# Epsilon inside the sum of squares, or added by ScalarE: the normalizations between and after the stages of a streaming-encoder block

## The chip, the cores and the metric

The kernel runs on one core of a Trainium2 chip. A core has TensorE (PE, matrix products into PSUM), VectorE (DVE), ScalarE (ACT), GpSimd (POOL), SyncE (SP, which here only starts DMA transfers), and 16 DMA engines. The metric is the time of one execution on the device in microseconds (us), as a median over runs; lower is better.

## The reference, cut to what matters

The reference is one residual block over 256 tokens of width 2048: a half-step SwiGLU network, a mixer, and another half-step SwiGLU network. After each of the three stands a normalization with gain and bias, and ahead of each a normalization without them, modulated by a vector that depends on the condition c.

```python
def _layer_norm(x, gain=None, bias=None):
    xf = x.astype(jnp.float32)
    mu = xf.mean(-1, keepdims=True)
    var = jnp.square(xf - mu).mean(-1, keepdims=True)
    y = (xf - mu) * lax.rsqrt(var + LN_EPS)
    ...
def modulate(h, s):
    return _layer_norm(h) * (1.0 + scale[:, s, None, :]) + shift[:, s, None, :]

y = _swiglu(modulate(x, 0), ffn1_w13[l], ffn1_w2[l])
x = _layer_norm(ALPHA * x + FFN_WEIGHT * gate[:, 0, None, :] * y, ln_g[l, 0], ln_b[l, 0])
u = modulate(x, 1)
...
x = _layer_norm(ALPHA * x + gate[:, 1, None, :] * y, ln_g[l, 1], ln_b[l, 1])
y = _swiglu(modulate(x, 2), ffn2_w13[l], ffn2_w2[l])
x = _layer_norm(ALPHA * x + FFN_WEIGHT * gate[:, 2, None, :] * y, ln_g[l, 2], ln_b[l, 2])
```

Each of these needs the reciprocal root of a variance plus epsilon (1e-5), one number for each token. The change is about who adds that epsilon.

## The kernel before, in words

The 256 tokens are two tiles of 128, one token to a partition; in the code `t` is 0 or 1, and `x[:, t, :]` holds a tile's 2048 columns. Weights stream in from memory as tiles of 128 by 2048, ScalarE and VectorE split each into a high and a low part, and TensorE multiplies the parts; this goes on almost without a gap from start to end. Each engine has a queue of its own that it works through in order. Around the places here the order in each queue is the order of the code: `V`, `A`, `G`, `T` and `Q` stand for VectorE, ScalarE, GpSimd, TensorE and SyncE and record every operation at one line of a helper, so that the profile shows L359 for all of them, and tiles have to be told by their names. The second SwiGLU network is laid out by a planner, but not its last part.

`boundary` (L577) makes the way from one stage to the next. It is called three times: after the first network (L1164, s = 0), after the mixer (L1928, s = 1) and at the very end (L1621, s = 2). The first two are **passages**: there `following` holds what the next stage needs. At the **end** `following` is None.

In it `norm(t)` (L616) makes a tile's normalization with gain and bias. VectorE turns statistics into mean and variance (`mv`, in the profile mvp), and `rstd_in_order` (L570) makes the factor `r` (rsp) on GpSimd in two instructions: an addition of epsilon (to the tile vep) and a power with the exponent -0.5. Meanwhile VectorE computes (x - mean) * gain for four quarters of 512 columns (L633). Then four instructions multiply by `r` and add the bias (L638, L644).

In a passage the modulated normalization follows at once and needs the mean and variance of what was just made. L638 sums each quarter into a column of the tile `sq`, and ScalarE sums the squares (L641). L649 adds up four columns each (tot), L651 makes the mean of it, and L652 makes mean squared minus mean square, the negated variance. `rstd_in_order` with the sign -1 turns it round and adds epsilon in one instruction (ven), and takes the power (rsn). With it `n_of` (L661) makes the normalized quarters n; TensorE transposes them (tu), ScalarE modulates them (u), VectorE makes a copy of the high part, and TensorE goes on with the next stage's products (o after the first passage, f after the second). While a tile's statistics are due, TensorE still has products of the other tile (tl), and ahead of the first transposes a `warm` product with tot as an operand.

At the end the second tile has a short cut for two of its four quarters (`early`): TensorE adds the products x * gain and -mean * gain in PSUM (tz), the second from a diagonal (dm) that ScalarE makes of the negated mean (nbn); L644 then reads tz in place of x. Each quarter is stored as soon as it is made (L645).

Of the kernel before, what the change touches and what calls it, by code (L numbers as in the profile page):

```python
# [11 lines left out]
F32 = mybir.dt.float32  # L12
F32R = mybir.dt.float32r
AF = mybir.ActivationFunctionType
ALU = mybir.AluOpType

P = 128
# [11 lines left out]
EPS = 1e-5  # L29
# [253 lines left out]
def block_kernel(ctx: ExitStack, tc: tile.TileContext, a: dict, out: bass.AP):  # L283
# [5 lines left out]
    sm = ctx.enter_context(tc.tile_pool(name="sm", bufs=4))  # L289
# [74 lines left out]
    V, A, G, T, Q = (Pinned(e) for e in (nc.vector, nc.scalar, nc.gpsimd, nc.tensor, nc.sync))  # L364
# [202 lines left out]
            A.mul(x[:, t, :], x[:, t, :], ALPHA)  # L567


    def rstd_in_order(var, nm, sign=1.0):  # L570
        v = sm.tile([P, 1], F32, tag="ve", name="ve" + nm)
        G.tensor_scalar(v, var, sign, EPS, op0=ALU.mult, op1=ALU.add)
        r = sm.tile([P, 1], F32, tag="rs", name="rs" + nm)
        G.tensor_tensor(r, v, mhalf, op=ALU.pow)
        return r

    def boundary(s, ps, hls, order, mm, sts, following, gated=False):  # L577
# [9 lines left out]
        if following:  # L587
            tiles, nm, ready, in_slots, fill, has_time, turn_at = following
# [27 lines left out]
        def norm(t, early={}):  # L616

            mv = sm.tile([P, 2], F32, tag="mv", name=f"mvp{s}{t}")
            V.bn_aggr(mv, sts[t].rearrange("p a b -> p (a b)"))
            r = rstd_in_order(mv[:, 1:2], f"p{s}{t}")  # L620

            sq = sums[t] = sm.tile([P, 2, 4], F32, tag="sq", bufs=2, name=f"sq{s}{t}")
            if early:
                nm_ = sm.tile([P, 2], F32, tag="nb", name=f"nbn{s}{t}")
                A.mul(nm_[:, 0:1], mv[:, 0:1], -1.0)
                diag = sm.tile([P, 512], F32, tag="gy", bufs=2, name=f"dm{s}{t}")[:, 0:P]
                A.activation(diag, ident, AF.Copy, scale=nm_[:, 0:1])
                for n in early:
                    T.matmul(early[n], diag, g[:, cs[n]], start=False, stop=True)
            for n, c in enumerate(cs):  # L630
                if n in early:
                    continue
                V.scalar_tensor_tensor(x[:, t, c], x[:, t, c], mv[:, 0:1], g[:, c], op0=ALU.subtract, op1=ALU.mult)  # L633
                yield
            for n in sorted(range(4), key=lambda n: n in early):
                c = cs[n]
                if following:
                    V.scalar_tensor_tensor(x[:, t, c], x[:, t, c], r, b[:, c], op0=ALU.mult, op1=ALU.add,  # L638
                                           accum_out=sq[:, 0, n:n + 1])
                    junk = sm.tile([P, 512], F32, tag="gy" if t else "u", bufs=2, name=f"junk{s}{t}{n}")  # L640
                    A.activation(junk, x[:, t, c], AF.Square, bias=sbs, scale=D ** -0.5,  # L641
                                 accum_out=sq[:, 1, n:n + 1])
                else:
                    V.scalar_tensor_tensor(x[:, t, c], early.get(n, x[:, t, c]), r, b[:, c], op0=ALU.mult, op1=ALU.add)  # L644
                    nc.sync.dma_start(out[t * P:(t + 1) * P, c], x[:, t, c])  # L645
                yield
            if following:
                tot = tots[t] = sm.tile([P, 4], F32, tag="tot", bufs=2, name=f"tot{s}{t}")
                V.tensor_reduce(tot[:, 0:2], sq, op=ALU.add, axis=mybir.AxisListType.X)  # L649

                V.tensor_scalar(tot[:, 2:3], tot[:, 0:1], 1.0 / D, sb, op0=ALU.mult, op1=ALU.add)  # L651
                V.scalar_tensor_tensor(tot[:, 3:4], tot[:, 2:3], tot[:, 2:3], tot[:, 1:2], op0=ALU.mult,  # L652
                                       op1=ALU.subtract)
                r = rstd_in_order(tot[:, 3:4], f"n{s}{t}", -1.0)
                nm_ = sm.tile([P, 2], F32, tag="nb", name=f"nbn{s}{t}")
                A.activation(nm_[:, 0:1], tot[:, 2:3], AF.Identity, bias=sb, scale=-1.0)
                A.activation(nm_[:, 1:2], nm_[:, 0:1], AF.Copy, scale=r)
                mrb[t] = nm_[:, 0:1], r, nm_[:, 1:2]
                yield
# [64 lines left out]
        mrb, sums, tots = {}, {}, {}  # L724
# [9 lines left out]
        if not following:  # L734
            run(norm(0))
            with tc.issue_after(end.ins):
                for n in early:
                    T.matmul(early[n], ident, x[:, 1, cs[n]], start=True, stop=False)
            run(takes(1, order[1]))
            run(norm(1, early))  # L740
            return

        A.activation(b, b, AF.Identity, accum_out=sb)
        A.mul(sb, sb, -1.0 / D)
        A.mul(sbs, sb, D ** -0.5)
        one = norm(0)
        other = chain(takes(1, order[1]), norm(1))

# [1326 lines left out]
```

## Time and profile before

| What | Value |
| --- | --- |
| median of 3 runs | 1861.64 us |
| lowest and highest of them | 1860.46 and 1862.16 us |
| the profiled execution | 1859.48 us |
| its span, first to last instruction | 1857.7 us |
| busy: TensorE, VectorE, ScalarE, GpSimd | 1842.9, 1610.5, 932.0, 66.2 us |
| granted TensorE clock, mean | 0.999 of full speed |
| instructions of GpSimd | 94 |
| memory traffic over the span | 294 GB/s |

The profile records the start and length of each instruction in one execution, counted from the start of the span. A row of its timeline has the start, the length, the engine, the source line, the instruction, the tile that it writes, and after the arrow those that it reads, with the count of equal instructions in a row. In brackets stands how long the engine had been idle and what released it. The chain of waits goes back from the last instruction, at each step to what came last before it; an engine's share of it says how much of the span hung on that engine. SCALAR_TENSOR_TENSOR is an instruction of VectorE with two tensors and a number for each partition. The first passage lies at about 740 to 812 us, the second at about 1126 to 1170 us, the end from about 1838 us on.

### The profile page before, as it was taken

Reading aid. Unit: us, or ns where it says so; the run is one execution under the profiler, and the core shown is the slowest. Engines: PE = TensorE matmul, PEld = TensorE weight load, DVE = VectorE, ACT = ScalarE, POOL = GpSimd, SP = SyncE. Lnnn points to the kernel's source line nnn. Section 1 sums busy time; section 2 is a strip of 40 time slices with the busy share of each in tenths; the row PEclk is TensorE's granted clock in tenths of the full one; section 3 lists DMA queues with packets and bytes.
Section 4 is the critical chain, followed back from the end, with each engine's and each line's share of the span. In section 5 each row is a group of like instructions: output and inputs, shape, how many; then the busy total and the mean of one; then the engine's idle time right before and its main releaser. Section 6 shows DMA issues by size and latency. Waiting matters only on the chain.

```text
span 1857.7 us, 21314 instructions
## 1 busy us (share of the span) xinstructions
PE 1842.9 (99%) x8423; PEld 1511.5 (81%) x8423; DVE 1610.5 (87%) x1506; ACT 932.0 (50%) x874; POOL 66.2 (4%) x94
## 2 busy tenths in 40 slices
PE   8999999999999999999999999999999999999998
PEld 5788888888888888788888887888888888888886
DVE  6899998888887986889997778899999989989886
ACT  4533444534333335564844346766565655665550
POOL 0000000000000000100000021000000000000000
PEclk9999999999999999999999999999999999999999
DMA  9999889999999897368678654888988888888852
GB/s 376 416 363 355 323 317 345 349 345 354 348 366 362 336 345 271 157 259 287 264 281 310 239 207 191 317 287 249 316 298 279 312 247 312 277 255 280 276 226 91
DMA packets 78677, 547.34 MB, mean 295 GB/s; under 512 B 9153, under 2 KB 9329, under 8 KB 13937
## 3 DMA queue, kind: packets, MB, share of 16 engines
q1 hardware_dynamic: 72144, 507.54, 71.2%
q0 software_dynamic: 4704, 34.63, 9.1%
q10 hardware_dynamic: 1728, 3.80, 0.6%
q8 instruction: 66, 1.08, 0.2%
q14 instruction: 35, 0.28, 0.0%
HBM read 541.72 MB, written 4.22 MB: 294 GB/s over the span
## 4 chain that ended last, share of the span: by engine, by line
PE 93%; DVE 3%; DMA 1%; ACT 1%; issue 1%; POOL 0%; POOLq 0%; DVEq 0%; SPq 0%; ACTq 0%
PE f L359 23%; PE py L359 9%; PE pj L507 6%; PE tl L359 4%; PE py L519 3%; PE py L520 3%; PE py L518 3%; PE pj L509 3%; PE fg L519 2%; PE fg L520 2%; PE fg L518 2%; PE fv L519 2%; PE fv L518 2%; PE fv L520 2%; PE rv L982 2%; PE rv L983 2%
## 5 line engine op out<-in xcount | busy, mean ns | idle before, releaser
L436 DVE CUSTOM_DVE_ANT_0 ada<-ada,scb,badac 128x2048 f32<-128x2048 f32 x94 | 220.4, 2345 | 21.3 <-DMA ada<-in_w_ada 21.1
L359 PE MATMUL py<-hw,ht 128*128 128x512 f32 x512 | 163.2, 390 | 0.0
L332 ACT CAST hra<-rra 128x2048 fp32r<-128x2048 f32 x38 | 72.6, 1915 | 102.2 <-DMA rra<-in_w_r 35.0
L332 ACT CAST hw<-rw 128x2048 fp32r<-128x2048 f32 x40 | 76.6, 1914 | 91.7 <-DMA rw<-in_w 46.9
L507 PE MATMUL pj<-u,hs 128*128 128x512 f32 x512 | 122.5, 391 | 0.0
L359 DVE CUSTOM_DVE_ANT_0 ada<-ada,scb,badac 128x2048 f32<-128x2048 f32 (+1 forms) x50 | 110.8, 2217 | 4.2 <-DMA ada<-in_w_ada 4.0
L359 PEld LDWEIGHTS py<-hw,ht 128*128 128x128 f32 x512 | 96.1, 188 | 19.8
L334 DVE TENSOR_TENSOR lw<-rw,hw 128x2048 fp32r<-128x2048 f32 x40 | 91.3, 2287 | 23.0 <-ACT hw L332 23.0
L507 PEld LDWEIGHTS pj<-u,hs 128*128 128x128 f32 x512 | 94.3, 188 | 18.4
L359 PE MATMUL py<-lw,ht 128*128 128x512 f32 x256 | 99.7, 389 | 0.7 <-DVE lw L359 0.7
L519 PE MATMUL py<-lw,hth 128*128 128x512 f32 x256 | 99.8, 390 | 0.1
L520 PE MATMUL py<-hw,htl 128*128 128x512 f32 x256 | 99.7, 390 | 0.0
L518 PE MATMUL py<-hw,hth 128*128 128x512 f32 x256 | 97.3, 392 | 0.0
L359 DVE TENSOR_TENSOR lw<-rw,hw 128x2048 fp32r<-128x2048 f32 x41 | 93.6, 2287 | 4.2 <-PE py L359 1.9
L332 ACT CAST hs<-rs 128x2048 fp32r<-128x2048 f32 x32 | 61.0, 1909 | 68.8 <-PE pj L507 63.6
L359 ACT CAST hw<-rw 128x2048 fp32r<-128x2048 f32 x41 | 78.4, 1911 | 32.8 <-DMA rw<-in_w 12.9
L334 DVE TENSOR_TENSOR ls<-rs,hs 128x2048 fp32r<-128x2048 f32 x32 | 73.0, 2280 | 11.4 <-ACT hs L332 11.4
L359 DVE TENSOR_TENSOR lra<-rra,hra 128x2048 fp32r<-128x2048 f32 x29 | 66.3, 2286 | 8.9 <-ACT hra L359 6.8
L509 PEld LDWEIGHTS pj<-u,ls 128*128 128x128 f32 x512 | 65.6, 191 | 2.5
L332 ACT CAST hfg<-rfg 128x2048 fp32r<-128x2048 f32 x20 | 38.3, 1916 | 57.6 <-DMA rfg<-in_w 57.6
L509 PE MATMUL pj<-u,ls 128*128 128x256 f32 x512 | 66.4, 283 | 0.0
L334 DVE TENSOR_TENSOR lfv<-rfv,hfv 128x2048 fp32r<-128x2048 f32 x20 | 45.8, 2290 | 21.2 <-ACT hfv L332 21.0
(794 smaller groups left out, 5023.2 us busy)
## 6 DMA issues: line engine op xcount, KB each, us to landing
ada<-in_w_ada SPq DMA_DIRECT2D x138, 1024.0 KB, 6.8
rw<-in_w SPq DMA_DIRECT2D x81, 1024.0 KB, 6.9
rfw<-in_w SPq DMA_DIRECT2D x56, 1024.0 KB, 7.2
rra<-in_w_r SPq DMA_DIRECT2D x45, 1024.0 KB, 7.5
rs<-in_w_s SPq DMA_DIRECT2D x32, 1024.0 KB, 5.1
rfw<-in_w POOLq DMA_DIRECT2D x26, 1024.0 KB, 9.2
rfv<-in_w SPq DMA_DIRECT2D x23, 1024.0 KB, 6.7
rfg<-in_w SPq DMA_DIRECT2D x20, 1024.0 KB, 6.4
```

The source lines that it names most:

```text
L332: act.copy(cut(hi, w), like(raw[:, w], hi))
L334: low.tensor_sub(cut(lo, w), like(raw[:, w], lo), cut(hi, w).bitcast(F32))
L359: self.last = getattr(self.engine, op)(*args, **kw)
L436: vec.tensor_tensor_reduce(raw[:, c], raw[:, c], scb[:, c], 1.0, base, ALU.mult, ALU.add, to)
L507: nc.tensor.matmul(ps, hi[:, k * P:(k + 1) * P], both(k), start=k == 0, stop=False)
L509: nc.tensor.matmul(ps[:, 0:S], lo[:, k * P:(k + 1) * P], uh[:, k, :], start=False, stop=k == KT - 1)
L518: pe.matmul(o, acth[:, k0 + j, tk], cut(hi, w), start=first and j == 0, stop=False, **kw)
L519: pe.matmul(o, acth[:, k0 + j, tk], cut(lo, w), start=False, stop=False, **kw)
L520: end = pe.matmul(o, actl[:, k0 + j, tk], cut(hi, w), start=False, stop=last and j == 3, **kw)
L982: pe.matmul(pss[t], uh[:, k0 + j, tk], hi[:, w], start=go, stop=False)
L983: pe.matmul(pss[t], uh[:, k0 + j, tk], lo[:, w], start=False, stop=False)
```

## The change

In a passage, `sq` gets a fifth column, filled by two GpSimd memsets: 0 beside the sums, epsilon beside the sums of squares. So the reduction brings epsilon in, the subtraction is turned round (`reverse1`) and gives the variance plus epsilon, and GpSimd only takes the power. For the first variance of a tile in a passage GpSimd still adds epsilon as before. At the end ScalarE adds it, by an ACTIVATE with a bias, and GpSimd only takes the power.

```diff
-    def rstd_in_order(var, nm, sign=1.0):
-        v = sm.tile([P, 1], F32, tag="ve", name="ve" + nm)
-        G.tensor_scalar(v, var, sign, EPS, op0=ALU.mult, op1=ALU.add)
+    def rstd_in_order(var, nm, eps=None):
+        v = var
+        if eps:
+            v = sm.tile([P, 1], F32, tag="ve", name="ve" + nm)
+            if eps is A:
+                A.activation(v, var, AF.Copy, bias=EPS)
+            else:
+                eps.tensor_scalar(v, var, 1.0, EPS, op0=ALU.mult, op1=ALU.add)
         r = sm.tile([P, 1], F32, tag="rs", name="rs" + nm)
         G.tensor_tensor(r, v, mhalf, op=ALU.pow)
         return r
...
-            r = rstd_in_order(mv[:, 1:2], f"p{s}{t}")
-
-            sq = sums[t] = sm.tile([P, 2, 4], F32, tag="sq", bufs=2, name=f"sq{s}{t}")
+            r = rstd_in_order(mv[:, 1:2], f"p{s}{t}", G if following else A)
+
+            sq = sums[t] = sm.tile([P, 2, 5], F32, tag="sq", bufs=2, name=f"sq{s}{t}")
+            if following:
+                G.memset(sq[:, 0, 4:5], 0.0)
+                G.memset(sq[:, 1, 4:5], EPS)
...
                 V.scalar_tensor_tensor(tot[:, 3:4], tot[:, 2:3], tot[:, 2:3], tot[:, 1:2], op0=ALU.mult,
-                                       op1=ALU.subtract)
-                r = rstd_in_order(tot[:, 3:4], f"n{s}{t}", -1.0)
+                                       op1=ALU.subtract, reverse1=True)
+                r = rstd_in_order(tot[:, 3:4], f"n{s}{t}")
```

The order of the built programs shows what moves. GpSimd in the first passage, before (the digits after a tile's letters are the passage and the token tile, then a running number):

```order
L359 TENSOR_SCALAR vep00_5100<-mvp00_5098 128x1
L359 TENSOR_TENSOR rsp00_5102<-vep00_5100,mhalf_78 128x1
L359 TENSOR_SCALAR ven00_5128<-tot00_5124 128x1
L359 TENSOR_TENSOR rsn00_5130<-ven00_5128,mhalf_78 128x1
L359 TENSOR_SCALAR vep01_5246<-mvp01_5244 128x1
L359 TENSOR_TENSOR rsp01_5248<-vep01_5246,mhalf_78 128x1
L359 TENSOR_SCALAR ven01_5273<-tot01_5269 128x1
L359 TENSOR_TENSOR rsn01_5275<-ven01_5273,mhalf_78 128x1
```

And GpSimd at the same place after the change:

```order
L359 TENSOR_SCALAR vep00_5100<-mvp00_5098 128x1
L359 TENSOR_TENSOR rsp00_5102<-vep00_5100,mhalf_78 128x1
L359 MEMSET sq00_5104 128x1 x2
L359 TENSOR_TENSOR rsn00_5130<-tot00_5126,mhalf_78 128x1
L359 TENSOR_SCALAR vep01_5246<-mvp01_5244 128x1
L359 TENSOR_TENSOR rsp01_5248<-vep01_5246,mhalf_78 128x1
L359 MEMSET sq01_5250 128x1 x2
L359 TENSOR_TENSOR rsn01_5275<-tot01_5271,mhalf_78 128x1
```

The additions into ven are gone and the power rsn reads tot; the memsets stand behind the power rsp. The second passage changes in the same way, and the only other difference there is that VectorE's reduction into tot now waits for GpSimd as well as for ScalarE.

GpSimd at the end of the program, as a piece of the difference (mvp, vep and rsp carry 2 for the end, then the token tile; the rows above are reloads of x):

```order
 L359 DMA yacc0_9108<-xd_121 128x2048
 L359 DMA yacc1_9114<-xd_121 128x2048
-L359 TENSOR_SCALAR vep20_13010<-mvp20_13008 128x1
 L359 TENSOR_TENSOR rsp20_13012<-vep20_13010,mhalf_78 128x1
-L359 TENSOR_SCALAR vep21_13033<-mvp21_13031 128x1
 L359 TENSOR_TENSOR rsp21_13035<-vep21_13033,mhalf_78 128x1
```

Both additions leave GpSimd. They come to ScalarE, again as a piece of the difference at the end of the program (ht and hil are parts of the last products' operands):

```order
 L359 CAST ht10_12783<-th101_12748 128x4x128
 L359 CAST hil0_12818<-rw22l0_12781 128x512 x4
+L359 ACTIVATE vep20_13010<-mvp20_13008 128x1
+L359 ACTIVATE vep21_13033<-mvp21_13031 128x1
 L359 ACTIVATE nbn21_13038<-mvp21_13031 128x1
 L359 ACTIVATE dm21_13040<-ident_73,nbn21_13038 128x128
```

There the second of them stands ahead of the negated mean and the diagonal. TensorE and SyncE keep their orders everywhere.

## The prediction

> **What bounds the kernel now.** I read the page first, then the chain of waits, then the timeline at the three places that the change touches, and last what TensorE waits for behind two of them. From the page, the span, the engines' busy time and the chain's shares by engine:
>
> ```profile
> span 1857.7 us, 21314 instructions
> ...
> PE 1842.9 (99%) x8423; PEld 1511.5 (81%) x8423; DVE 1610.5 (87%) x1506; ACT 932.0 (50%) x874; POOL 66.2 (4%) x94
> ...
> PE 93%; DVE 3%; DMA 1%; ACT 1%; issue 1%; POOL 0%; POOLq 0%; DVEq 0%; SPq 0%; ACTq 0%
> ```
>
> TensorE is the bound: 93% of the chain. GpSimd is 0% of it, rounded, so what can be won from GpSimd is a few times a microsecond at most, and only where the chain runs through it. The chain of waits (start, length, what) names it in two places. At the first passage, and then at the end:
>
> ```profile
> 760.13 0.57 POOL ven L359
> ...
> 760.77 0.56 POOL rsn L359
> ```
>
> ```profile
> 1848.67 0.27 DVE mvp L359
> ...
> 1849.02 0.75 POOL vep L359
> ...
> 1849.81 0.99 POOLq L2071
> ...
> 1850.82 1.41 DVE yacc L359 x2
> ```
>
> Here "POOLq" is the power itself. A naive reading takes 0.57 us and its hand-over, 0.07, off the first place, and most of 0.75 off the second. The chain names only the releaser that came last, though, so each place has to be looked at for what came second.
>
> **Step 1: the end, second token tile.** The timeline (start, length, engine, instruction, and in brackets the idle time and its releaser):
>
> ```profile
> 1840.80 2.74 DVE L359 SCALAR_TENSOR_TENSOR yacc<-yacc,mvp,ln_g 128x512 f32<-128x512 f32 x4
> ...
> 1843.45 2.73 DVE L359 SCALAR_TENSOR_TENSOR yacc<-yacc,rsp,ln_b 128x512 f32<-128x512 f32 x4
> ...
> 1848.96 0.20 ACT L359 ACTIVATE nbn<-mvp 128x1 f32<-128x1 f32 x1 [36.39 <-DVE mvp L359]
> 1848.96 1.42 DVE L359 SCALAR_TENSOR_TENSOR yacc<-yacc,mvp,ln_g 128x512 f32<-128x512 f32 x2
> 1849.02 0.75 POOL L359 TENSOR_SCALAR vep<-mvp 128x1 f32<-128x1 f32 x1 [6.38 <-DVE mvp L359]
> ...
> 1849.65 1.98 PE L359 MATMUL tz<-ln_g,dm 128*128 128x512 f32 x4 [0.76 <-ACT dm L359]
> 1849.85 0.94 POOL L359 TENSOR_TENSOR rsp<-vep,mhalf 128x1 f32<-128x1 f32 x1
> ...
> 1850.82 1.41 DVE L359 SCALAR_TENSOR_TENSOR yacc<-yacc,rsp,ln_b 128x512 f32<-128x512 f32 x2 [0.44 <-POOL rsp L359]
> 1852.15 1.40 DVE L359 SCALAR_TENSOR_TENSOR yacc<-tz,rsp,ln_b 128x512 f32<-128x512 f32 x2
> ```
>
> VectorE steps through such instructions every (1843.45 - 1840.80) / 4 = 0.66 us. Its two subtractions therefore leave it free at 1848.96 + 2 x 0.66 = 1850.29, and it stood until 1850.82 for the power: 0.53 us is all that this place can give, whatever GpSimd does.
>
> Does the power come by 1850.29 now? The mean and variance are there at 1848.94 (1848.67 + 0.27). ScalarE was idle and took the same kind of instruction from the same releaser at 1848.96 in 0.20 us, so the sum with epsilon is there at 1849.16; with 0.08 for the hand-over (1848.94 to 1849.02 above) GpSimd can begin at 1849.24. It then meets VectorE's first subtraction, which has two inputs in SBUF. The rows show what that does: the addition here takes 0.75 us and ends 0.15 after VectorE's first step (1849.62), and the power ends at 1850.79, 0.50 after the second (1850.29). With VectorE out of the way the two take 0.19 and 0.55, as the second passage shows below. So GpSimd waits for the end of VectorE's instruction and then does its work. The new power: 1849.62 + 0.50 = 1850.12, or 0.17 before VectorE is free. VectorE then goes on at 1850.29: a gain of **0.53 us**, and VectorE itself is late next.
>
> What the detour costs: the negated mean (nbn) and the diagonal (dm) stand behind the new ScalarE instruction, 0.20 later, so TensorE's products into tz end at 1849.65 + 1.98 + 0.20 = 1851.83. The last instruction on tz would start at 1850.29 + 3 x 0.66 = 1852.27, the first on the earlier bank 0.66 before. 0.44 is left over: hidden. The four stores go with VectorE, each 0.53 earlier. For the first token tile the same edit is worth nothing: VectorE is busy with the four subtractions to 1843.45, then with the four scalings, and waits for TensorE afterwards.
>
> Does GpSimd's work in turn hold up VectorE? The four at 1840.80, with an addition and a power beside them, took 2.74 us, and the four at 1843.45 without either took 2.73: VectorE loses nothing. The Trainium skill ("SBUF — State Buffer", section "SBUF: two separate sides") speaks against this: it calls the port pair that VectorE and GpSimd share an exclusive lock, and whichever starts first has it for the whole instruction. The trace agrees as far as GpSimd waits, and disagrees on VectorE; by the rule this place would give 0.04 in place of 0.53 (rival C).
>
> **Step 2: the first passage, first token tile.** Timeline:
>
> ```profile
> 759.37 0.16 DVE L359 TENSOR_REDUCE tot<-sq 128x2 f32<-128x8 f32 x1 [0.44 <-ACT junk L359]
> ...
> 759.82 0.22 DVE L359 SCALAR_TENSOR_TENSOR tot<-tot 128x1 f32<-128x1 f32 x1
> ...
> 759.96 0.68 DVE L359 TENSOR_TENSOR x<-x,gy 128x512 f32<-128x512 f32 x1
> 760.13 0.56 POOL L359 TENSOR_SCALAR ven<-tot 128x1 f32<-128x1 f32 x1 [5.39 <-DVE tot L359]
> ...
> 760.67 0.69 DVE L359 BATCH_NORM_STATS2 sts<-x 128x6 f32<-128x512 f32 x1
> 760.77 0.55 POOL L359 TENSOR_TENSOR rsn<-ven,mhalf 128x1 f32<-128x1 f32 x1
> 761.36 1.00 DVE L359 TENSOR_SCALAR n<-x,nbn,rsn 128x512 f32<-128x512 f32 x2
> ...
> 761.96 1.18 PE L359 MATMUL tu<-ident,n 128*128 128x128 f32 x8 [0.33 <-DVE n L359]
> ```
>
> The chain names GpSimd, but n has no idle time before it: VectorE's own statistics end at 760.67 + 0.69 = 761.36. And the addition's 0.56 is mostly a wait for the addition of x (ends 760.64); the power would now meet the same wait and end at 760.64 + 0.50 = 761.14 in place of 761.32. So GpSimd is 0.18 earlier and VectorE is not, but for an overlap: a pair of 1.42 with a step of 0.66 makes 0.76 for one, so the next may start 0.10 before its end. On the other side, the reduction now waits for ScalarE and for GpSimd's memsets, a second wait; the bound for that is 0.05, above the 0.04 that n needs after the power (761.32 to 761.36) with three engines to wait for. Value taken: **0**, ends -0.10 and +0.05.
>
> **Step 3: the second passage, first token tile.**
>
> ```profile
> 1147.20 0.19 POOL L359 TENSOR_SCALAR ven<-tot 128x1 f32<-128x1 f32 x1 [5.41 <-DVE tot L359]
> ...
> 1147.47 0.55 POOL L359 TENSOR_TENSOR rsn<-ven,mhalf 128x1 f32<-128x1 f32 x1
> ...
> 1148.06 1.46 DVE L359 TENSOR_SCALAR n<-x,nbn,rsn 128x512 f32<-128x512 f32 x3 [0.95 <-POOL rsn L359]
> ...
> 1148.16 1.02 PE L359 MATMUL f<-gate,tot 128*128 128x512 f32 x2
> ...
> 1149.02 1.04 PE L359 MATMUL tu<-ident,n 128*128 128x128 f32 x8
> ```
>
> Here the addition's 0.19 and its hand-over, 0.27 in all (1147.47 - 1147.20), do come off VectorE's wait. But the transposes (tu) follow TensorE's two warming products without a gap, at 1149.02, while n's first quarter is ready at 1148.06 + 1.46 / 3 = 1148.55. TensorE comes last: **0**.
>
> **Step 4: the second token tiles of both passages.** What TensorE waits for in 763 to 812 us, and in 1150 to 1243:
>
> ```profile
> PE o L359 <- DVE u L359: 0.3, 1, 0.3
> ```
>
> ```profile
> PE f L359 <- DVE u L359: 0.4, 1, 0.4
> ```
>
> Both waits are those of the first token tiles (u); TensorE waits for nothing of the second ones, so the 0.27 that goes there lies beside its products: **0**.
>
> **Step 5: the added memsets.** They stand behind the power and ahead of nothing but the next power, which is due 5 us later. A one-column memset and the place:
>
> ```profile
> 0.86 0.10 POOL L382 MEMSET mhalf<- 128x1 f32 x1
> ```
>
> ```profile
> 752.90 2.74 DVE L359 SCALAR_TENSOR_TENSOR x<-x,mvp,ln_g 128x512 f32<-128x512 f32 x4
> ...
> 753.79 0.95 POOL L359 TENSOR_TENSOR rsp<-vep,mhalf 128x1 f32<-128x1 f32 x1
> ...
> 755.56 0.75 DVE L359 SCALAR_TENSOR_TENSOR x<-x,rsp,ln_b 128x512 f32<-128x512 f32 x1
> ```
>
> The power ends at 754.74, the reduction needs the zeros and epsilons at 759.37. Two memsets are 0.2 us alone, and 1.5 if each met VectorE as an addition does (0.75): either way over 3 us of cover. The scalings wait for the power's count, not for the memsets. The reduction over 10 columns for 8 and the reversed subtraction keep their instruction. **0**.
>
> **The sum.** 0.53 + 0 + 0 + 0 + 0: the profiled execution would go from 1859.48 (span 1857.7 and 1.8 around it) to 1858.95. It lies 2.2 under the median of the runs, 1861.64, so against that median I say **1861.1**.
>
> **The rivals.**
> A, the forecast: -0.53, 1861.1.
> B, GpSimd bounds the first passage after all, as its chain says: n comes as much earlier as TensorE stood for it, 0.33 of the 0.64. For it speaks the chain; against it the statistics that end at 761.36. -0.53 - 0.33: 1860.8.
> C, the shared port takes back the end: VectorE's second subtraction waits while the power runs, from 1849.62 to 1850.12, so that VectorE is free at about 1850.78: -0.04, 1861.6. Against it the row of 2.74.
> D, slower: the way over ScalarE. If its sum reaches GpSimd after 1849.62 (over 0.38 later than worked out), the power gets in at 1850.29 only, ends at 1850.79, and nothing is won; from there each later tenth is lost in full. The longest thing that could stand there is a load of ScalarE's tables:
>
> ```profile
> L359 ACT ACT_TABLE_LOAD x1 | 1.3, 1283 | 0.0
> ```
>
> With 1.28 ahead of it the sum comes at 1850.44, the power ends free of VectorE at 1850.52 + 0.55 = 1851.07, and VectorE goes on 0.28 late: 1861.9. Against it: the program's order has as many table loads after the change as before, and none near the end.
> E, the change does not do what its words say: in the passages GpSimd still adds epsilon to the first of the two variances of each tile; that is in the terms above. What stays is that the order of the whole shifts for a reason that I do not see.
>
> **How the numbers follow.** A 0.62, B 0.08, C 0.18, D 0.07, E 0.05. The four runs of before lie from 1859.48 to 1862.16; half of that, 1.34, goes below B and above D: **1859.4 to 1863.2**. No case but E moves the time by 0.2%, 3.7 us, which is about what a measurement of this kernel can tell from no change; E's 0.05 is split: faster 0.02, same 0.95, slower 0.03.
>
> **What would show it.** Right: at the end an eps instruction of ScalarE of 0.2 us, a power of 0.8 to 0.9 us that starts about 0.3 after the mean, and no idle time of VectorE before its scalings; in the first passage n still directly behind the statistics, with the power of about 1.0 us beside the addition of x; in the second a transpose still behind the warming products. Wrong: VectorE idle at the end (D), its pair of subtractions at 1.9 us in place of 1.42 (C), TensorE's 0.33 gone in the first passage (B), or a wait of the reduction on GpSimd.

## The result, and the profile after

| What | Before | After |
| --- | --- | --- |
| median (5 runs each, on one chip) | 1861.64 us | 1876.17 us |
| lowest and highest | 1860.46 and 1862.89 us | 1875.79 and 1878.29 us |
| ratio after to before, 95% interval | | 1.0081 [1.0070, 1.0092] |
| the profiled execution, its span | 1859.48, 1857.7 us | 1876.17, 1874.4 us |

The change makes the kernel slower by 0.8%, 14.5 us. The forecast was a gain of 0.5 us and a range up to 1863.2: it was wrong.

The page of the kernel after has the span, the engines' busy time and the shares of the chain:

```profile
span 1874.4 us, 21322 instructions
...
PE 1860.3 (99%) x8423; PEld 1511.9 (81%) x8423; DVE 1611.3 (86%) x1506; ACT 931.7 (50%) x876; POOL 64.2 (3%) x96
...
PE 92%; issue 3%; DVE 2%; DMA 2%; ACT 1%; DVEq 0%; POOL 0%; SPq 0%; ACTq 0%; POOLq 0%
```

The span grew by 16.7 us and TensorE's busy time by 17.4 (1842.9 to 1860.3), with the same 8423 products. The other engines' busy time has hardly changed. So the loss isn't a wait: TensorE takes longer over the same work. (The profiled execution of before lay 2.2 under its median and that of after on its median, which is why spans differ by 16.7 and medians by 14.5.)

**The three places do what was predicted.** Here is the end of after, second token tile, in the timeline (start, length, engine, instruction, in brackets the idle time and its releaser):

```profile
1865.86 0.26 DVE L359 BATCH_NORM_AGGREGATE mvp<-sts 128x2 f32<-128x24 f32 x1
1866.16 0.20 ACT L359 ACTIVATE vep<-mvp 128x1 f32<-128x1 f32 x1 [8.15 <-DVE mvp L359]
1866.16 1.42 DVE L359 SCALAR_TENSOR_TENSOR yacc<-yacc,mvp,ln_g 128x512 f32<-128x512 f32 x2
1866.27 0.19 ACT L359 ACTIVATE nbn<-mvp 128x1 f32<-128x1 f32 x1
1866.44 0.88 POOL L359 TENSOR_TENSOR rsp<-vep,mhalf 128x1 f32<-128x1 f32 x1 [7.46 <-ACT vep L359]
...
1866.94 1.98 PE L359 MATMUL tz<-ln_g,dm 128*128 128x512 f32 x4 [0.85 <-ACT dm L359]
1867.49 1.41 DVE L359 SCALAR_TENSOR_TENSOR yacc<-yacc,rsp,ln_b 128x512 f32<-128x512 f32 x2
1868.81 1.41 DVE L359 SCALAR_TENSOR_TENSOR yacc<-tz,rsp,ln_b 128x512 f32<-128x512 f32 x2
```

From the first subtraction to the first scaling it is 1867.49 - 1866.16 = 1.33 us, where before had 1850.82 - 1848.96 = 1.86. That is the predicted 0.53, and VectorE has no idle time ahead of the scaling. The first passage of after:

```profile
765.47 0.16 DVE L359 TENSOR_REDUCE tot<-sq 128x2 f32<-128x10 f32 x1 [0.51 <-ACT junk L359]
...
766.05 0.68 DVE L359 TENSOR_TENSOR x<-x,gy 128x512 f32<-128x512 f32 x1
766.21 0.93 POOL L359 TENSOR_TENSOR rsn<-tot,mhalf 128x1 f32<-128x1 f32 x1 [5.37 <-DVE tot L359]
766.77 0.69 DVE L359 BATCH_NORM_STATS2 sts<-x 128x6 f32<-128x512 f32 x1
767.38 0.99 DVE L359 TENSOR_SCALAR n<-x,nbn,rsn 128x512 f32<-128x512 f32 x2
```

The power meets the addition of x and takes 0.93 in place of 0.55; n still stands directly behind VectorE's own statistics. And the second passage of after:

```profile
1154.37 0.55 POOL L359 TENSOR_TENSOR rsn<-tot,mhalf 128x1 f32<-128x1 f32 x1 [5.39 <-DVE tot L359]
...
1154.95 1.46 DVE L359 TENSOR_SCALAR n<-x,nbn,rsn 128x512 f32<-128x512 f32 x3 [0.67 <-POOL rsn L359]
...
1155.44 1.02 PE L359 MATMUL f<-gate,tot 128*128 128x512 f32 x2
...
1156.30 1.04 PE L359 MATMUL tu<-ident,n 128*128 128x128 f32 x8
```

VectorE's wait fell from 0.95 to 0.67, and the transposes still follow TensorE's warming products without a gap.

**Where the 17 us come from.** First, when. GpSimd's first instruction of the first passage, in before and then in after:

```profile
752.96 0.74 POOL L359 TENSOR_SCALAR vep<-mvp 128x1 f32<-128x1 f32 x1 [161.52 <-DVE mvp L359]
```

```profile
758.98 0.74 POOL L359 TENSOR_SCALAR vep<-mvp 128x1 f32<-128x1 f32 x1 [164.79 <-DVE mvp L359]
```

This instruction is unchanged and stands ahead of every changed one, and it is already 6.0 us late. At the start of the end (VectorE's four subtractions, 1840.80 in before) the lag is 17.0:

```profile
1857.81 2.74 DVE L359 SCALAR_TENSOR_TENSOR yacc<-yacc,mvp,ln_g 128x512 f32<-128x512 f32 x4
```

At the last tile's it is 17.2 (1848.96 to 1866.16). Taking off the 0.53 won there leaves the 16.7 by which the span grew. Nearly all of the loss thus lies in stretches of the program where no instruction was changed.

Second, what. The stretch from 300 to 400 us, with its length, then the busy time and count of TensorE, its weight loads, VectorE, ScalarE and GpSimd, then the granted TensorE clock, the share of the DMA engines and GB/s; in before and then in after:

```profile
300.00:400.00 100.00, 100.00 (x451) 82.82 (x450) 85.27 (x83) 47.43 (x37) 0.00 (x0) 1.00 0.95 355
```

```profile
300.00:400.00 100.00, 100.00 (x441) 80.97 (x440) 85.53 (x83) 47.36 (x37) 0.00 (x0) 1.00 0.93 352
```

TensorE is full in both, at full clock in both, and does 441 products in place of 451. GpSimd does nothing there. Third, which products. Groups (busy time, mean ns of one) of before and then of after:

```profile
L519 PE MATMUL py<-lw,hth 128*128 128x512 f32 x256 | 99.8, 390 | 0.1
...
L518 PE MATMUL fg<-hfg,u 128*128 128x512 f32 x160 | 59.4, 391 | 0.0
```

```profile
L519 PE MATMUL py<-lw,hth 128*128 128x512 f32 x256 | 101.4, 396 | 0.0
...
L518 PE MATMUL fg<-hfg,u 128*128 128x512 f32 x160 | 59.4, 391 | 0.0
```

The products of the first network's second half (hth holds the activations, lw a weight tile's low part) take 6 ns more each, those of its first half (u, hfg) not a nanosecond. The products overlap, so the better measure is the step from one start to the next in the trace: for py<-lw,hth it went from 226.8 to 233.4 ns, for fg<-lfg,u only from 226.8 to 227.3.

So something tells the operand hth from the operand u. In the built programs it is the address. A partition's share of `sq` grew from 2 x 4 to 2 x 5 numbers, 32 to 40 bytes. Buffers there start at multiples of 32 bytes, so each of the two now takes 64 (they start at 176128 and 176160 before, at 176128 and 176192 after), and every tile laid out behind them has moved by 64 bytes:

| Tiles | First address in a partition, before | After | Modulo 256 |
| --- | --- | --- | --- |
| six large slots: hth, htl, part of the second network's weights | 177056 | 177120 | 160, now 224 |
| streamed weights, high and low parts | 117152 to 158112 | the same | 160 |
| u of the first network | 51616 | the same | 160 |

Before, moving operand (the 512 columns that stream) and stationary operand (the 128 columns that are loaded) lay alike modulo 256 in the products of all these tiles. After, those with one operand in a slot don't.

### The profile page after: what moved, and what is told of

Its sections match the earlier page's. It is cut to its first block, busy times and chain, and to the rows that moved or that the text cites. A ratio compares the mean times of both kernels' runs of the same rounds, so it can differ in the third digit from the quotient of the medians.

```text
span 1874.4 us, 21322 instructions
## 1 busy us (share of the span) xinstructions
PE 1860.3 (99%) x8423; PEld 1511.9 (81%) x8423; DVE 1611.3 (86%) x1506; ACT 931.7 (50%) x876; POOL 64.2 (3%) x96
## 4 chain that ended last, share of the span: by engine, by line
PE 92%; issue 3%; DVE 2%; DMA 2%; ACT 1%; DVEq 0%; POOL 0%; SPq 0%; ACTq 0%; POOLq 0%
PE f L359 21%; PE py L359 9%; PE pj L507 5%; PE tl L359 4%; PE py L519 3%; PE py L520 3%; PE py L518 3%; PE pj L509 3%; PE fg L519 2%; PE fg L520 2%; PE fg L518 2%; PE fv L519 2%; PE fv L518 2%; PE fv L520 2%; PE rv L990 2%
## 5 line engine op out<-in xcount | busy, mean ns | idle before, releaser
L436 DVE CUSTOM_DVE_ANT_0 ada<-ada,scb,badac 128x2048 f32<-128x2048 f32 x94 | 220.4, 2345 | 17.4 <-DMA ada<-in_w_ada 17.1
```

Of the source, the lines that this page charges most:

```text
L436: vec.tensor_tensor_reduce(raw[:, c], raw[:, c], scb[:, c], 1.0, base, ALU.mult, ALU.add, to)
```

## The experiments

**Theory (place):** the size of `sq` moves the slots, and a product is slower when its two operands don't lie alike modulo some power of two. **Rival (instructions):** what GpSimd, ScalarE and VectorE now do, or their changed order, costs TensorE time. The changed lines can't have run before 6 us are lost, but the whole program is built anew, so this was to be tried. Two kernels part the two. In each table and row below "before" is the kernel before, run on the same chip beside the others.

**Only the size.** The kernel before, with `sq` cut from a larger tile; no instruction is changed:

```diff
-            sq = sums[t] = sm.tile([P, 2, 4], F32, tag="sq", bufs=2, name=f"sq{s}{t}")
+            sq = sums[t] = sm.tile([P, 2, 5], F32, tag="sq", bufs=2, name=f"sq{s}{t}")[:, :, 0:4]
```

> The kernel before, with the tile sq one column wider and the fifth column never used: no instruction is changed, but the tiles allocated after sq lie 64 bytes further on. Place theory (the slots moved against the streamed weight tiles, and products with one operand in each step slower): 1876.7 us, the time after the change plus the 0.5 that the end gives. Instruction theory (the added or moved instructions cost it): 1861.6, as before.

Measured: 1876.23 us (1876.03 to 1876.42) against 1860.90, a ratio of 1.0080 [1.0066, 1.0094]. Groups and the stretch from 300 to 400 us of this kernel:

```profile
L519 PE MATMUL py<-lw,hth 128*128 128x512 f32 x256 | 101.4, 396 | 0.0
```

```profile
300.00:400.00 100.00, 100.00 (x440) 81.01 (x439) 85.36 (x83) 47.31 (x37) 0.00 (x0) 1.00 0.92 351
```

The whole loss is there, with the same 396 ns, and nothing of the change was made but the eight bytes.

**All of the change, without the size.** The kernel after, with `sq` and `tot` of a token tile in one tile of 16 numbers, 64 bytes, as the two took before. The slots, the weights and u lie where they lay before; only about a dozen tiles of a few columns have changed places, since ven is gone:

```diff
-            sq = sums[t] = sm.tile([P, 2, 5], F32, tag="sq", bufs=2, name=f"sq{s}{t}")
+            both_ = sm.tile([P, 16], F32, tag="sq", bufs=2, name=f"sq{s}{t}")
+            sq = sums[t] = both_[:, 0:10].rearrange("p (a b) -> p a b", a=2)
...
-                tot = tots[t] = sm.tile([P, 4], F32, tag="tot", bufs=2, name=f"tot{s}{t}")
+                tot = tots[t] = both_[:, 10:14]
```

> The changed kernel, with sq and tot in one tile of 64 bytes, so that every later tile lies where it lay before the change; the instructions are those of the change. Place theory: 1861.1 us, 0.5 under before, which is the sum that was predicted; products of py at 227 ns a step. Instruction theory: 1876.2, as after the change.

Measured: 1861.07 us (1859.24 to 1862.95, 11 runs) against 1860.90 (15 runs), a ratio of 1.0001 [0.9992, 1.0009]. Its groups, and its end in the timeline:

```profile
L519 PE MATMUL py<-lw,hth 128*128 128x512 f32 x256 | 99.8, 390 | 0.1
```

```profile
1852.32 1.42 DVE L359 SCALAR_TENSOR_TENSOR yacc<-yacc,mvp,ln_g 128x512 f32<-128x512 f32 x2
...
1852.60 0.88 POOL L359 TENSOR_TENSOR rsp<-vep,mhalf 128x1 f32<-128x1 f32 x1 [7.27 <-ACT vep L359]
...
1853.65 1.41 DVE L359 SCALAR_TENSOR_TENSOR yacc<-yacc,rsp,ln_b 128x512 f32<-128x512 f32 x2
```

The products are back at 390 ns and the loss is gone. The 0.53 at the end is there (1853.65 - 1852.32 = 1.33), but 0.03% can't be told from nothing within runs that lie 3.7 us apart. So this is the change as it was priced, and it is worth no time that can be measured. The instruction rival falls.

**Which shift costs how much.** All of the following are the kernel before with small tiles enlarged or merged, so that only addresses differ. Slots 32 bytes up:

```diff
-            sbt = sm.tile([P, 2], F32, tag="sb", bufs=1, name=f"sb{s}")
+            sbt = sm.tile([P, 10], F32, tag="sb", bufs=1, name=f"sb{s}")
```

> The kernel before, with the slots moved by 32 bytes (a wider tile sb, its columns unused). Place theory in the form that what matters is whether the two operands of a product have the same address modulo 128: slower than before, anywhere from 1865 to 1885 us. In the form that only modulo 64 matters, 32 is worse than 64: over 1877. In the form that only an odd multiple of 64 does harm: 1861.6. Instruction theory: 1861.6.

Slots 128 bytes down, by two tiles (statistics, mean and variance) cut from one:

```diff
-                st = sm.tile([P, 6], F32, tag="hst", name="hst" + nm)
+                hm = sm.tile([P, 8], F32, tag="hst", name="hst" + nm)
+                st = hm[:, 0:6]
...
-                mv = sm.tile([P, 2], F32, tag="hmv", name="hmv" + nm)
+                mv = hm[:, 6:8]
```

> The kernel before, with two small statistics tiles of the mixer's heads merged, so that the slots lie 128 bytes lower. Place theory modulo 128: 1861.6 us, as before, though the slots moved. If the modulus is 256 or any move does harm: 1870 or more.

Slots 64 bytes down: the merge above, and `sbt` of 18 numbers:

> The kernel before, with the slots 64 bytes lower in place of 64 higher. Relation theory with the sizes of the products measured alone: 1734 products with the stationary operand in a slot and the moving one in a weight tile at 229.0 ns in place of 226.7, 4.0 us; 487 the other way round at 233.3, 3.2 us; some 2 us for the products between them: 1867 to 1871 us, so clearly less than the 15 us of 64 bytes the other way. If only the size of the shift counts, not its sign: 1876.

Slots 256 bytes down: the merge above, and in the same way `hve` and `rd` in one tile of two numbers:

> The kernel before, with four small tiles of the mixer's heads merged into two, so that the slots lie 256 bytes lower; 128 bytes cost 1873.0. If the relation of the operands counts modulo 256: 1860.9 us. If modulo 512 or if any distance from the old place costs: 1868 or more.

Everything 64 bytes up, so that the slots lie where the change puts them but the two operands keep their relation:

```diff
-    mhalf = cst.tile([P, 1], F32, name="mhalf")
+    mhalf = cst.tile([P, 24], F32, name="mhalf")[:, 0:1]
```

> The kernel before, with everything from the third small constant on moved by 64 bytes (a wider constant, its columns unused): activations, weight tiles and slots move together. If it is the relation of the two operands that costs: 1860.9 us, as before, at 227 ns a product. If it is where the slots lie by themselves: 1876 or more, since now the other operands lie off too.

Measured, with the mean step of the products whose moving operand lies in an unmoved tile and whose next stationary operand lies in a slot (where everything moved, and in before, of nearly all):

| Slots moved by | Stationary less moving, modulo 256 | Mean step, ns | Median, us | Ratio to before |
| --- | --- | --- | --- | --- |
| nothing (before) | 0 | 227.1 | 1860.90 | |
| +64 (after) | 64 | 233.2 | 1876.17 | 1.0081 [1.0070, 1.0092] |
| +32 | 32 | 233.2 | 1875.65 | 1.0077 [1.0062, 1.0093] |
| -128 | 128 | 232.6 | 1872.96 | 1.0062 [1.0048, 1.0076] |
| -64 | 192 | 229.1 | 1868.90 | 1.0044 [1.0027, 1.0060] |
| -256 | 0 | 227.1 | 1861.09 | 1.0005 [0.9995, 1.0015] |
| all tiles by +64 | 0 | 227.3 | 1861.98 | 1.0008 [0.9998, 1.0017] |

(The befores beside them: 1861.64 for the change, 1861.27 for -64, 1860.74 for the last two.) The groups, in the order +32, -128, -64, -256, all by +64:

```profile
L519 PE MATMUL py<-lw,hth 128*128 128x512 f32 x256 | 101.4, 396 | 0.0
```

```profile
L519 PE MATMUL py<-lw,hth 128*128 128x512 f32 x256 | 101.2, 395 | 0.0
```

```profile
L519 PE MATMUL py<-lw,hth 128*128 128x512 f32 x256 | 100.3, 392 | 0.0
```

```profile
L519 PE MATMUL py<-lw,hth 128*128 128x512 f32 x256 | 99.8, 390 | 0.1
```

```profile
L519 PE MATMUL py<-lw,hth 128*128 128x512 f32 x256 | 99.8, 390 | 0.1
```

What follows, one form of the place theory at a time. 32 bytes cost about as much as 64, so "alike modulo 64" (over 1877 expected) and "only odd multiples of 64" (1861.6) are refuted. 128 bytes cost, so "alike modulo 128" is refuted. 256 bytes cost nothing, so the modulus is 256. All tiles by 64 cost nothing that the interval can tell, so it isn't the place of the slots itself but the relation of the two operands. And the size isn't simply growing with the shift: 64 bytes down cost half of 64 bytes up. That case had been worked out beforehand from the steps that the next kernel gave (1867 to 1871), and 1868.90 lies inside; one term of it was off, the 487 products the other way round, which took 231.7 ns and not 233.3.

**TensorE by itself.** What stays is whether the loss needs the rest of the kernel: the stream of weights, VectorE and ScalarE on the same tiles. This kernel computes nothing of the reference. It makes products alone, 32 for each pair of shifts: `mov` streams 512 columns, `sta` is loaded 128 columns at a time, and either is shifted in steps of 32 bytes, or both alike. The part of it that makes the products of one pair of shifts:

```python
def cell(bank, i, j, times):
    for n in range(times):
        m0 = 512 * (n % 4) + STEP * i
        s0 = 256 * (n % 8) + STEP * j
        nc.tensor.matmul(bank, sta[:, s0:s0 + P], mov[:, m0:m0 + 512], start=n == 0, stop=n == times - 1)
```

> TensorE alone: 32 products at a time of a stationary tile of 128 columns and a moving one of 512, both shifted by a number of 32-byte steps from places that are equal modulo 1024. It computes nothing of the reference. If the two operands' relation costs by itself: 227 ns a product at shift 0 and wherever both shift alike, 231 to 236 at the others, and back to 227 at the modulus (256 or 512 bytes). If the cost comes only with other engines' and the DMA's traffic: 227 everywhere.

It ran once, 659.39 us. From its page, its groups and the stretch from 100 to 600 us:

```profile
PE 644.5 (98%) x2784; PEld 523.9 (80%) x2784; DVE 8.0 (1%) x10; ACT 5.1 (1%) x3; POOL 0.2 (0%) x4
```

```profile
L39 PE MATMUL ps<-mov,sta 128*128 128x512 f32 x2784 | 644.5, 394 | 7.6 <-ACT mov L31 7.6
```

```profile
100.00:600.00 500.00, 500.00 (x2163) 405.97 (x2163) 0.00 (x0) 0.00 (x0) 0.00 (x0) 1.00 0.00 1
```

No other engine works in that stretch, the DMA share is 0.00 and the clock 1.00. The mean step with the stationary operand shifted, from the trace, without the first and last two of each 32:

| Stationary less moving, modulo 256 | 0 | 32 | 64 | 96 | 128 | 160 | 192 | 224 |
| --- | --- | --- | --- | --- | --- | --- | --- | --- |
| Mean step, ns | 226.7 | 233.4 | 233.3 | 234.3 | 232.4 | 233.2 | 229.0 | 233.3 |

The row repeats every 256 bytes up to 1024, and with the moving operand shifted in place of the stationary one it comes out within 1.2 ns of it. At 192 it is lower than expected (231 to 236). It holds the kernel's own values: 233.2 at 64, 233.2 at 32, 232.6 at 128 and the odd one, 229.1 at 192. So the loss needs only TensorE and the places of its two operands: no other engine and no transfer ran beside it. The Trainium skill ("SBUF — State Buffer", section "SBUF: two separate sides") says of SBUF's engine ports that "only the shared port pair causes contention" and that TensorE never waits on anyone. That is about waiting for other engines, and no run here speaks against it there; but by the grid TensorE alone goes 3% slower by where its own operands lie.

Why it does, the runs don't show. Two values look odd beside the row, and the traces settle one. The products with both operands shifted alike should all give 226.7, and gave 228.0 on average. The excess lies at the borders, where for one product the moving operand has the old shift and the next stationary one the new: the first ten products behind a border took 230.9, the other 21 of the 31 steps 226.7. So such a border can be felt for ten products behind it. The kernel after shows the same. Of its products with neither operand in a slot, 1078 have one with an operand in a slot among the ten ahead of them; their mean step went from 227.4 in before to 231.0. The mean of the others stayed at 227.2.

The second value stays open: in the kernel after, the 487 products that stream from a slot while the next load is from an unmoved tile (stationary less moving 192) took 231.8, where the grid has 229.0. They mostly stand alone or in pairs among other products, and not 32 in a row as in the grid; whether that is the reason, no run shows.

## Why the prediction was wrong, step by step

**The step that failed** is Step 5, in its last words: "The reduction over 10 columns for 8 and the reversed subtraction keep their instruction. 0." The fifth column was priced as an instruction, and as an instruction it is free. It wasn't priced as a tile. The 8 bytes became 64 in each of the layout's addresses behind it, and the size of what that cost by the after trace's products of 512 columns is: 1734 with the next load in a slot x (233.2 - 227.1) = 10.6 us, 487 the other way round x (231.8 - 227.1) = 2.3, 141 with both in slots x (230.0 - 227.1) = 0.4, and 4785 with neither x (228.0 - 227.1) = 4.3. Together 17.6, beside 17.4 that TensorE was busy longer. The last term is the after-effect: the 1078 products behind those with an operand in a slot make 3.8 us of it.

From it the sum was wrong by 15 us, and with it "No case but E moves the time by 0.2%". E was the only case that allowed for so much, but for a reason that didn't come true, a shifted order: in the built programs each engine's order is that of before but for the change itself. An order names tiles and says nothing of where they lie.

**Step 1**, the end: right to the hundredth, 0.53. The power takes 0.88 and starts 0.32 after the mean (1865.86 + 0.26 to 1866.44). It ends at 1867.32, 0.17 before VectorE is free, as worked out. The negated mean came 0.11 later, not 0.20, since ScalarE's two instructions overlap. **Rival C** is refuted by the pair of subtractions at 1.42 with the power beside it, **rival D** by the scaling without idle time.

**Step 2**, the first passage: right. The power beside the addition of x took 0.93 where 1.01 was worked out (from the addition's start), n started 0.61 after the statistics did in place of 0.69, inside the end of -0.10. The reduction's idle time grew from 0.44 to 0.51, a little over the bound of 0.05 for the second wait. **Rival B** is refuted: n stands behind VectorE's statistics.

**Step 3**, the second passage: right. 0.28 came off VectorE's wait (0.95 to 0.67), and the transposes still wait for the warming products. **Step 4**, the second token tiles: right as far as TensorE's waits show it. In the two passages of after it waits once for u, 0.3 and 0.4 us, as before, and for nothing of the second tiles. With the layout kept, the whole of the change comes to 0.0001 of the time [-0.0008, 0.0009], in sum no more than 1.7 us either way.

So every line of "What would show it" for the right case can be found in the trace of after, and the time was 15 us off. A prediction that lists the changed instructions and finds each of them where it was expected hasn't yet covered the unchanged ones.

## What to carry to other kernels

A change that alters a tile's size, by however little, is two changes: the one in the diff, and a new address for everything laid out behind it. Compare the addresses of both operands of the busiest products before and after, and keep the layout as it was (by padding, or by merging small tiles) while the change itself is timed. In a profile a moved layout shows as products that go slower at the same clock, ahead of the first changed instruction, some groups by a few nanoseconds each and others not at all.

## What the runs showed of the hardware that was not expected

- The step of 512-column products depends on the relation of stationary and moving operand modulo 256 bytes: 226.7 ns when alike, 229.0 at 192, 232.4 to 234.3 at the other multiples of 32. That is 3% of a product, and 0.8% of this kernel though only about a quarter of its products had such a pair.
- The effect outlasts its cause: in the grid the first ten products behind a border took 230.9 ns though their own operands lay alike, the others 226.7.
- It doesn't take another engine or a transfer: in the grid DMA stood at 0.00 and all engines but TensorE at none.
- GpSimd's one-column power waits for VectorE's instruction with two inputs (0.88 to 0.93 us against 0.55 alone), but the VectorE instruction behind isn't held up by it (the pair took 1.42 us with it and without it 1.41).
